# Second half of the tokens in a hybrid attention layer: four column pairs of the input projection in seven block products, the other twelve columns cut into pieces of three matmuls

## The chip, the cores and the metric

The kernel runs on one core of one Trainium2 chip. The metric is the device time of one execution in microseconds (us). Before the change it is 2535.86 us, the median of three runs (2535.32 to 2537.22). One further execution was recorded by the hardware profiler; it took 2533.9 us, of which the recorded span of the program is 2532.2 us.

The engines are named as the profile names them: PE is TensorE (matmuls), PEld its weight loads, DVE is VectorE, ACT is ScalarE, POOL is GpSimd, SP is SyncE, which here only issues DMAs.

## What is computed

One layer of a streaming encoder over 2048 tokens of width 1024, in float32. The parts that matter here:

```python
u = rms_norm(h, g_mix_pre)                      # 2048 x 1024
z = u @ w_in                                    # 1024 x 2816: 22 column blocks of 128
qa, ka, va, qh, fh, ih, gh = split(z, IN_SPLITS)
ya = swa_with_sinks(qa, ka, va, sinks)          # sliding window of 128, 8 heads of 64, sink logits
yh = hgrn2(qh, fh, ih, gh, lb, onorm)           # gated recurrence, 4 heads of 128, chunks of 64
y  = concatenate([ya, yh]) @ w_out
h  = h + rms_norm(y, g_mix_post)
# cross-attention into 256 memory tokens, then a SwiGLU FFN of width 2816, each with its norms
```

In the attention of each head, the softmax runs over the window's scores and one further logit, the sink.

## The kernel before

Every large product is split in three: each float32 operand is the sum of a rounded high part and a low part, and a product is high x high, high x low and low x high. So a block of 128 columns, 1024 deep, for 512 tokens, is 8 x 3 = 24 matmuls of 128x512.

**Stage 1** (`in_first`, lines 471 to 628) normalises the input and projects the first 1024 tokens. Two columns of `w_in` (a pair, from the table `ORDER`) form a 2x2 block problem with the two halves of the depth and the two halves of the tokens. The method `seven` (line 1202) does it in seven products of 12 matmuls instead of eight. It needs seven combinations of the token operand, called T and numbered 1 to 7 (8 where the product is a plain one), each stored as high and low parts in SBUF, and seven combinations of the weights, called S, which `streamed` (line 1132) makes for each pair. The seven T stand in seven slots: four in the pool `big`, three in the pool `t2`. `phases` (line 1286) is the loop over pairs: for each product (a step) it records the matmuls, the results' epilogue, the next S and, where a new set of T is due, half a T at a time. `split2` (line 1027) makes a high part on ACT or POOL and the low part on DVE (line 1038).

After the eleven pairs, stage 1 loads the second 1024 tokens' `u`, splits it into four tiles `u1` (no combinations), and projects one pair, columns 4 and 5 (the keys and values of the attention), plainly, in 96 matmuls.

**The mixing stage** follows. It runs three things side by side: the sliding-window attention `swa` for 16 blocks of 128 tokens, n = 0 to 15; the recurrence `hgrn` for the first 8 blocks; and `in_proj` (line 737), which projects the remaining 20 columns for the second half of the tokens, one column of 48 matmuls after another (`in_cols`, tiles `psg`, `whi`, `wlo`). `swa_front(n)` (line 816) loads queries (`qs`), keys (`kk`) and values (`vr`), makes four banks of scores, and the softmax; `swa_back(n)` (line 882) transposes the probabilities (tile `S` by `ident`), splits them (`pth`, `ptl`) and multiplies by the values. `hgrn_front` writes `atz`, `kt`, `vt`; the tile `W` is the recurrence's state. The back of n-1 is recorded after the front of n. The order of instructions on each engine is set when the program is built, by a list scheduler that knows priorities (the order of recording) and its own estimate of durations; on the chip each engine takes its queue strictly in that order. Columns of `in_proj` are recorded one per block, so the scheduler drops their matmuls wherever it sees PE free.

`kk` has two buffers: the keys of n+1 can be loaded while the scores of n still read theirs. The loads are issued by SP in the order of its queue.

The sink enters the softmax as follows: the row's minimum of the negated scores and the negated sink is taken on DVE (line 864), the exponentials and their sum on ACT (line 868); the sink's own exponential takes one POOL addition (line 871), one ACT exponential (line 872) and another POOL addition (line 874) before DVE takes the reciprocal (line 876).

**The later stages**: the fold of the cross-attention's weights, which runs beside the second half of `hgrn`, then the output projection, cross-attention and FFN, all as `phases` of seven products.

## Time and profile before

| what | value |
|---|---|
| median of three runs | 2535.86 us |
| the profiled execution | 2533.9 us |
| its span | 2532.2 us |
| PE busy | 2493.8 us, 98% of the span, 11942 matmuls |
| DVE busy | 1749.1 us, 69% |
| ACT busy | 1240.7 us, 49% |
| POOL busy | 365.4 us, 14% |
| stage 1 ends, first `psg` matmul of the mixing stage | 269.0 us |
| first score matmul of the mixing stage | 282.1 us |
| last `psg` matmul | 633.0 us |

The span is the time from the first to the last instruction of the program; the execution's own time is 1.7 us longer. A matmul's record overlaps with the next one's, because matmuls are pipelined, so "busy" does not say that PE runs at its peak; the number of matmuls in a window divided by its length says that better. The PE clock that the chip granted is in a column of its own, 1.00 for full speed.

### The profile page before, as it was taken

The page shows a single profiled execution, that of the slowest core. Times are in us where ns is not written, and L with a number is a line of the kernel's source. Part 1 is how long each engine was busy: PE and PEld are TensorE (multiplying, and loading weights), DVE is VectorE, ACT ScalarE, POOL GpSimd, SP SyncE. Part 2 cuts the span into 40 slices and gives each one's busy share as a digit, 9 for nine tenths or more (in the row PEclk, how much of TensorE's full clock was granted, in tenths as well). Part 3 has the DMA queues.
Part 4 walks back from the last instruction along what each step waited for, and adds up shares of the span by engine and source line. Part 5 has one row for each costly group of instructions (what it writes and reads, how often), then busy time and mean ns, then how long its engine had stood idle before and what let it go on. Part 6 is the DMA issues. An engine that isn't in the chain of part 4 may idle for free.

```text
span 2532.2 us, 33939 instructions
## 1 busy us (share of the span) xinstructions
PE 2493.8 (98%) x11942; PEld 2084.7 (82%) x11942; DVE 1749.1 (69%) x2787; ACT 1240.7 (49%) x2582; POOL 365.4 (14%) x540
## 2 busy tenths in 40 slices
PE   9999999999999999999999999999999999999998
PEld 8778888888987788878878888888888888888886
DVE  8896477865556989988866655576566557574766
ACT  5463356654565576566753333353333335443543
POOL 4241244321400111112200000000000000000122
PEclk9999999999999999999999999999999999999999
DMA  7544877785887996858944322254354334565777
GB/s 221 158 158 164 239 198 178 223 270 135 278 298 266 302 335 194 255 175 255 339 164 169 136 76 93 78 196 154 129 208 167 117 127 156 177 184 110 231 169 156
DMA packets 313403, 483.56 MB, mean 191 GB/s; under 512 B 21904, under 2 KB 198032, under 8 KB 313232
## 3 DMA queue, kind: packets, MB, share of 16 engines
q1 hardware_dynamic: 304880, 455.17, 54.1%
q0 software_dynamic: 8352, 26.22, 6.1%
q8 instruction: 94, 1.54, 0.2%
q14 instruction: 77, 0.63, 0.1%
HBM read 305.15 MB, written 176.16 MB: 190 GB/s over the span
## 4 chain that ended last, share of the span: by engine, by line
PE 83%; DVE 5%; DMA 5%; issue 2%; ACT 2%; POOL 1%; SPq 1%; DVEq 0%; POOLq 0%; ACTq 0%
PE psm L1200 22%; PE psm L1198 22%; PE psm L1199 22%; PE psg L158 2%; PE psg L156 2%; PE psg L157 2%; DVE S L1038 1%; DMA y_d<-ys 1%; DVE T L1038 1%; DMA raw<-in_wo_x_dram 1%; DVE sum L1173 0%; DMA pair<-in_x_dram 0%; DMA out_s<-u 0%; SPq L75 0%; ACT junk L1569 0%
## 5 line engine op out<-in xcount | busy, mean ns | idle before, releaser
L1198 PE MATMUL psm<-T,S 128*128 128x512 f32 x2680 | 1034.4, 391 | 12.6 <-ACT part L1213 8.4
L1199 PE MATMUL psm<-T,S 128*128 128x512 f32 x2680 | 1042.6, 390 | 1.2 <-DVE T L1038 1.1
L1200 PE MATMUL psm<-T,S 128*128 128x512 f32 x2680 | 1030.0, 390 | 5.0 <-DVE S L1038 5.0
L1198 PEld LDWEIGHTS psm<-T,S 128*128 128x128 f32 x2680 | 503.1, 188 | 124.8 <-ACT part L1213 13.0
L1200 PEld LDWEIGHTS psm<-T,S 128*128 128x128 f32 x2680 | 503.4, 188 | 112.4 <-DVE S L1038 8.4
L1199 PEld LDWEIGHTS psm<-T,S 128*128 128x128 f32 x2680 | 503.5, 188 | 106.7 <-DVE T L1038 3.0
L1035 ACT ACTIVATE S<-sum 128x512 fp32r<-128x512 f32 (+1 forms) x370 | 224.1, 619 | 374.8 <-PE psm L1200 270.4
L1038 DVE TENSOR_TENSOR S<-sraw,S 128x512 fp32r<-128x512 f32 (+1 forms) x315 | 212.0, 679 | 236.9 <-ACT S L1035 233.7
L1213 ACT ACTIVATE part<-psm 128x512 f32<-128x512 f32 x285 | 168.6, 596 | 253.1 <-PE psm L1200 237.8
L1038 DVE TENSOR_TENSOR S<-sum,S 128x512 fp32r<-128x512 f32 (+1 forms) x388 | 258.0, 673 | 43.9 <-ACT S L1035 40.0
L1035 ACT ACTIVATE S<-sraw 128x512 fp32r<-128x512 f32 (+1 forms) x300 | 184.5, 618 | 110.7 <-PE psm L1200 108.7
L1602 POOL DMA_DIRECT2D y_d<-row x16 | 14.0, 872 | 1077.3 <-DVE row L1784 1015.3
L1038 DVE TENSOR_TENSOR T<-row,T 128x1024 fp32r<-128x1024 f32 (+1 forms) x112 | 130.8, 1183 | 28.3 <-ACT T L1035 26.4
L156 PE MATMUL psg<-u,whi 128*128 128x512 f32 x320 | 127.6, 399 | 0.7 <-DVE z L770 0.5
L157 PE MATMUL psg<-u,whi 128*128 128x512 f32 x320 | 127.3, 398 | 0.0
L158 PE MATMUL psg<-u,wlo 128*128 128x512 f32 x320 | 126.7, 397 | 0.0
L1569 ACT ACTIVATE junk<-row 128x512 f32<-128x512 f32 x160 | 99.6, 624 | 46.3 <-DVE row L1591 19.9
L1035 ACT ACTIVATE T<-row 128x1024 fp32r<-128x1024 f32 (+1 forms) x112 | 113.4, 1031 | 10.6 <-DMA row<-d_s 5.3
L1735 DVE TENSOR_TENSOR row<-psm,part 128x512 f32<-128x512 f32 x66 | 44.0, 687 | 71.3 <-PE psm L1200 71.3
L1038 DVE TENSOR_TENSOR wlo<-raw,whi 128x1024 fp32r<-128x1024 f32 x52 | 65.4, 1258 | 36.0 <-ACT whi L1035 30.9
L1784 DVE TENSOR_TENSOR row<-psm,part 128x512 f32<-128x512 f32 x72 | 49.1, 687 | 49.3 <-PE psm L1200 49.2
L1744 DVE TENSOR_TENSOR part<-psm,part 128x512 f32<-128x512 f32 x66 | 43.7, 687 | 52.2 <-PE psm L1200 52.2
(355 smaller groups left out, 3476.2 us busy)
## 6 DMA issues: line engine op xcount, KB each, us to landing
sraw<-in_w_gate_dram SPq DMA_DIRECT2D x44, 512.0 KB, 3.8
sraw<-in_w_up_dram SPq DMA_DIRECT2D x44, 512.0 KB, 3.6
hid_d<-row SPq DMA_DIRECT2D x44, 512.0 KB, 2.6
sraw<-hid_d SPq DMA_DIRECT2D x32, 512.0 KB, 4.6
sraw<-in_w_in_dram SPq DMA_DIRECT2D x48, 256.0 KB, 3.9
raw<-in_w_in_dram SPq DMA_DIRECT2D x20, 512.0 KB, 6.3
row<-in_w_down_dram SPq DMA_DIRECT2D x20, 512.0 KB, 7.3
row<-d_s SPq DMA_DIRECT2D x20, 512.0 KB, 8.4
```

Source lines behind the costliest of these rows:

```text
L156: nc.tensor.matmul(ps, ah, bh, start=(i == 0), stop=False)
L157: nc.tensor.matmul(ps, ah, bl, start=False, stop=False)
L158: nc.tensor.matmul(ps, al, bh, start=False, stop=(i == n - 1))
L1035: self.nc.scalar.activation(hi, raw, AF.Copy)
L1038: self.nc.vector.tensor_tensor(lo, raw, f32(hi), ALU.subtract)
L1198: nc.tensor.matmul(ps, s[:, 0, k, :], t[:, 0, k, :], start=st, stop=False, **kw)
L1199: nc.tensor.matmul(ps, s[:, 0, k, :], t[:, 1, k, :], start=False, stop=False, **kw)
L1200: nc.tensor.matmul(ps, s[:, 1, k, :], t[:, 0, k, :], start=False, stop=sp, **kw)
L1213: nc.scalar.activation(t, ps, AF.Copy)
L1569: self.nc.scalar.activation(junk, a, AF.Square, scale=float(D) ** -0.5, accum_out=to)
L1735: nc.vector.tensor_tensor(d, a, c, ALU.add)
L1784: nc.vector.tensor_tensor(d, a, b, ALU.add)
```

## The change

Nothing of what the layer computes is changed. Five things are:

1. In stage 1 the second half of the tokens becomes a second job of `phases` with the first five pairs of `ORDER` (`MORE = 5`): columns (4,5), (0,1), (2,3) and (10,6) in seven products each, (11,7) in eight. For that the T of the second half are made: the generator `sums` loads the four blocks of `u` and makes three of the combinations in place on DVE, `operand` hands them to `split2` and makes the last. Each new T takes the slot of the first job's T of the same number. Blocks (0,1) and (1,1) are loaded a second time.
2. `in_proj` keeps twelve columns (12, 8, 13, 9, 14 to 21). It yields after each three matmuls (one step of depth: high x high, high x low, low x high); a method `fill(n)` records n such pieces, each bound to issue after the PE instruction recorded last. 32 pieces run before the mixing stage's first block; then 1 to 2 pieces stand behind each of the four score groups and 2 behind the transposes of each head group. A column's weights are loaded one column ahead.
3. The softmax: the masked scores go to four fixed tiles `scores`, with the negated sink in an extra last column, so the exponential and its sum on ACT include the sink; the POOL additions and the extra exponential are gone.
4. Buffers: `kk` has one buffer instead of two, `qs` three instead of four, `ys` is named with two.
5. The accumulating DMA of the attention's output (POOL queue) is issued one block later.

The core of the diff, with whole hunks left out:

```diff
-                cols = self.in_proj(1, u)
-                next(cols)
-                for _ in range(NPB + 1):
+                cols = self.cols = self.in_proj(1, u)
+                for _ in range(32):
+                    next(cols)
+                self.fills = (1, 1, 1, 1, 2, 2)
+                for i in range(NPB + 1):
                     next(swa)
                     next(hgrn)
-                    next(cols)
+                self.fills = (1, 2, 2, 1, 2, 2)
...
+        more = [("p" if i == self.MORE - 1 else "s",) + self.in_block(*p, 1, (), [], (), False, None)
+                for i, p in enumerate(self.ORDER[:self.MORE])]
...
+        def sums():
+            for k, at in ((7, (1, 1)), (5, (0, 1)), (1, (0, 0)), (2, (1, 0))):
+                second[k] = fetched(*at)
+                yield
+            for d, a, b, op in ((7, 7, 5, ALU.subtract), (5, 5, 1, ALU.subtract), (6, 1, 7, ALU.add)):
...
+                for k in (0, 2):
+                    kk = slice(k, k + 2)
+                    nc.vector.tensor_tensor(second[d][:, kk], second[a][:, kk], second[b][:, kk], op)
+                    yield
+        def operand(i, j, a, n):
+            key = i if j is None else {v: k for k, v in self.BLOCK.items()}[i, j]
+            if key in (3, 8) and not a:
+                second[key] = fetched(i, j)
+            if key == 4:
+                return second[2][:, a:a + n], second[6][:, a:a + n]
+            return second[key][:, a:a + n]
...
-        phases = self.phases([(lambda i, j, a, n: raw[i, j][:, a:a + n, :], 4, blocks, None, {})], T)
+        phases = self.phases([(lambda i, j, a, n: raw[i, j][:, a:a + n, :], 4, blocks, None, {len(blocks) - 2: [sums]}),
+                              (operand, 4, more, True, {})], T)
...
-        for s in range(2):
-            u.append([])
-            for q in range(2):
-                t = self.big.tile([P, 2, 4, 512], F32R, tag="big", name=f"u1_{q}{s}")
...
-                self.mm3(ps, [((S[i + k // 4 * 2][:, 0, k % 4, :], S[i + k // 4 * 2][:, 1, k % 4, :]), u[s][k])
-                              for k in range(KT)])
+        T = {k[1]: t for k, t in T.items() if type(k) is tuple and k[0]}
+        return [[(T[p][:, 0, k, :], T[p][:, 1, k, :]) for p in ps for k in range(4)] for ps in ((1, 2), (8, 3))]
...
+    def fill(self, n):
+        for _ in range(n):
+            with self.queued(self.traced(mybir.EngineType.PE)):
+                next(self.cols, None)
...
-                self.mm3(ps, [((w[i][0][:, k, :], w[i][1][:, k, :]), u[s][k]) for k in range(KT)])
+            for k, (bh, bl) in enumerate(u[s]):
+                ah, al = w[0][:, k, :], w[1][:, k, :]
+                nc.tensor.matmul(ps, ah, bh, start=(k == 0), stop=False)
+                nc.tensor.matmul(ps, ah, bl, start=False, stop=False)
+                nc.tensor.matmul(ps, al, bh, start=False, stop=(k == KT - 1))
+                if k < KT - 1:
+                    yield
...
-            q = ph.tile([P, 4, P], F32R, tag="qs", name=f"qs{n}_{g}", bufs=4)
+            q = ph.tile([P, 4, P], F32R, tag="qs", name=f"qs{n}_{g}", bufs=3)
...
-        kk = ph.tile([P, 2, 2, M], F32R, tag="kk", name=f"kk{n}", bufs=2)
+        kk = ph.tile([P, 2, 2, M], F32R, tag="kk", name=f"kk{n}", bufs=1)
...
+                self.fill(self.fills[2 * g + i2])
...
-            se = self.small("w_se", 4)
-            nc.gpsimd.tensor_tensor(se, self.sink[:, 4 * g:4 * g + 4], mn, ALU.add)
-            nc.scalar.activation(se, se, AF.Exp)
-            dn = self.small("w_dn", 4)
-            nc.gpsimd.tensor_tensor(dn, den, se, ALU.add)
             rd = self.small("w_rd", 4)
-            nc.vector.reciprocal(rd, dn)
+            nc.vector.reciprocal(rd, den)
...
+            self.fill(self.fills[4 + g])
...
+                if first and queue[0][0]:
+                    free = next(s for s in slots if s[2] == where[queue[0][1]])
```

How the change moves instructions is shown at two places. The first is DVE's queue at the end of stage 1, where the T of the second half come in. The first row, `pair<-psm,part` of line 694, is the epilogue of product 3 of the first job's last pair, the same work in both kernels (line 685 in the changed one). Before, this is what stands behind it (the `u` row is two halves of a tile):

```order
L694 TENSOR_TENSOR pair_2169<-psm_2118,part_2150 128x512
L1038 TENSOR_TENSOR u_01_2242<-pair_1948,u_01_2242 128x1024 x2
L1038 TENSOR_TENSOR S_2261<-sraw_2252,S_2261 128x512
L707 SCALAR_TENSOR_TENSOR pair_2169<-th_2171,pair_2169 128x512
L694 TENSOR_TENSOR pair_2169<-psm_2096,part_2131 128x512
```

In the changed kernel the same epilogue row opens a stretch of 26 rows, up to the first half of T_2302, the tile of product 2, the sixth of the seven. Its end reads:

```order
L1038 TENSOR_TENSOR T_2222<-pair_2223,T_2222 128x1024
L1038 TENSOR_TENSOR S_2384<-sraw_2104,S_2384 128x512
L1178 TENSOR_TENSOR sum_2474<-sraw_2275,sum_2451 128x512
L1038 TENSOR_TENSOR T_2222<-pair_2223,T_2222 128x1024
L1038 TENSOR_TENSOR S_2366<-sraw_2104,S_2366 128x512
L1038 TENSOR_TENSOR T_2271<-pair_1972,T_2271 128x1024
L1038 TENSOR_TENSOR T_2302<-pair_2037,T_2302 128x1024
```

On PE, that tile is asked for by the 57th matmul counted from the second job's first (twelve of these still belong to the first job's last product), ahead of the last ones of product 3 (T_2222):

```order
L1205 MATMUL psm_2303<-T_2222,S_2320 128x512
L1203 MATMUL psm_2303<-T_2222,S_2320 128x512
L1203 MATMUL psm_2278<-T_2271,S_2343 128x512
L1203 MATMUL psm_2390<-T_2302,S_2366 128x512
L1204 MATMUL psm_2303<-T_2222,S_2320 128x512
```

So nine halves of T stand in this stretch of DVE's queue, where before it held halves of `u` tiles, and on PE single products now ask for them in turn.

The second place is SP's queue in the mixing stage, at the loads for one block of attention (`kk` is loaded in two halves of 64 partitions, `qs_0` and `qs_1` are the queries of the two head groups; the brackets name what a row waits for, PE or an earlier transfer). Before, at n = 3, the query load waits for PE, the key load for no engine:

```order
L75 DMA raw_3922<-in_w_in_dram 128x1024 [waits DMAHW0_49,DVE_49]
L75 DMA qs_1_3170<-zq_d 64x4x128 [waits DMAHW1_49,PE_49]
L75 DMA qs_1_3170<-zq_d 64x4x128 [waits DMAHW2_49]
L75 DMA kk_3173<-zk_d 64x4x256 [waits DMAHW3_49]
L75 DMA kk_3173<-zk_d 64x4x256 [waits DMAHW4_49]
L75 DMA qq_3339<-z_d 128x4x128 [waits DMAHW5_49,PE_49]
```

In the changed kernel, at n = 10, the key load itself waits for PE, that is for the last score matmul of n = 9, which reads the only `kk` buffer:

```order
L75 DMA sg_5066<-z_d 128x4x128 [waits DMAHW4_49,DMAHW1_49]
L75 DMA qs_1_5272<-zq_d 64x4x128 [waits DMAHW5_49,PE_49]
L75 DMA qs_1_5272<-zq_d 64x4x128 [waits DMAHW6_49]
L75 DMA kk_5275<-zk_d 64x4x256 [waits DMAHW7_49,PE_49]
L75 DMA kk_5275<-zk_d 64x4x256 [waits DMAHW0_49]
L75 DMA qs_0_5437<-zq_d 64x4x128
L78 DMA y_d<-sg_5066 128x512 [waits DMAHW2_49,DVE_49]
```

PE's queue behind those scores holds what is left of block n = 9 before the first score of the next block. The end of that stretch, for n = 10 to n = 11 (`pth`, `ptl` by `vst` are the value products, `vr` the transposed values):

```order
L899 MATMUL psh_5395<-pth_00_5376,vst_4915 128x512
L899 MATMUL psh_5426<-pth_10_5406,vst_4915 128x512
L900 MATMUL psh_5395<-ptl_00_5377,vst_4915 128x512
L899 MATMUL psh_5395<-pth_01_5385,vst_5121 128x512
L840 MATMUL pss_5448<-ident,vr_5446 128x128
L900 MATMUL psh_5395<-ptl_01_5386,vst_5121 128x512
L859 MATMUL pst_5456<-kk_5443,qs_0_5437 128x256
```

Between the last score of one block and the first of the next there are now, on PE, only the pieces and the back of the block before; a load that starts at the one has to land before the other.

More of the change, by code (lines that the diff above doesn't have):

```diff
@@ L250, in prologue @@
                             next(phases)
-                next(cols)
+                for _ in range(8):
+                    next(cols, None)
                 next(fold)
@@ L662, in stream, with out @@
         def stream(kind):
-            for _ in range(3):
-                next(iter(get), None)
             return self.streamed(load, 4, kind)
-        def out(i, j, a, b):
+        def out(i, j, a, o):
             c0 = (ca, cb)[i] * P
@@ L737, in in_proj @@
     def in_proj(self, b, u):
-        order = [c for p in self.ORDER for c in p]
+        order = [c for p in self.ORDER for c in p][2 * self.MORE:]
         e1 = None
-        for c in order[2:]:
-            e1 = self.in_cols(b, u, [c], e1)
+        w = self.wcols(self.I["w_in"], order[0] * P)
+        for c, d in zip(order, order[1:] + [None]):
+            cur = self.in_cols(b, u, c, e1, w)
+            next(cur)
             yield
-    def in_cols(self, b, u, cols, e1):
+            if d is not None:
+                w = self.wcols(self.I["w_in"], d * P)
+            e1 = yield from cur
@@ L1302, in phases @@
         held = 7 if first else -1
-        slots = [("A", -2, i) for i in range(4)] + [("B", held if i == 2 else -1, i) for i in range(3)]
-        T, keep = {}, [{} for _ in jobs]
+        slots = [("A", -2, i) for i in range(4)] + [("B", held if i == 6 else -1, i) for i in range(4, 7)]
+        T, keep, where = {}, [{} for _ in jobs], {}
         current, left = [None], {}
@@ L1346, in half @@
                 n, p, _ = k = queue.pop(0)
+                where[p] = free[2]
                 slots.remove(free)
```

165 lines of the change are left out of this document (72 added, 93 removed).

## The prediction

> **What bounds the kernel now.** I read the page first, for the busy shares and the chain that ended last.
>
> ```profile
> span 2532.2 us, 33939 instructions
> PE 2493.8 (98%) x11942; PEld 2084.7 (82%) x11942; DVE 1749.1 (69%) x2787; ACT 1240.7 (49%) x2582; POOL 365.4 (14%) x540
> PE 83%; DVE 5%; DMA 5%; issue 2%; ACT 2%; POOL 1%; SPq 1%; DVEq 0%; POOLq 0%; ACTq 0%
> ```
>
> PE is the bound: 83% of the chain is PE. So a matmul that is left out is worth its pitch, the time from one start to the next, as long as nothing else comes to end last. I then cut the span into windows, for that pitch and for the stages that the change touches (columns: window, its length, then busy time and instruction count of each engine, granted PE clock, share of the DMA engines, GB/s).
>
> ```profile
> core 0: us, PE busy (x) PEld busy (x) DVE busy (x) ACT busy (x) POOL busy (x), PEclk, DMA share, GB/s
> 1300.00:1650.00 350.00, 350.00 (x1546) 289.92 (x1545) 201.46 (x304) 125.03 (x221) 0.00 (x0) 1.00 0.32 112
> 110.00:115.00 5.00, 1.98 (x7) 1.64 (x8) 5.00 (x7) 3.94 (x6) 0.86 (x3) 0.94 0.43 105
> 115.00:120.00 5.00, 5.00 (x18) 3.97 (x17) 3.03 (x5) 1.12 (x2) 1.12 (x2) 0.72 0.27 80
> 224.20:269.00 44.80, 44.24 (x195) 36.32 (x194) 26.75 (x37) 17.30 (x25) 8.53 (x11) 1.00 0.50 164
> 269.00:300.00 31.00, 30.53 (x168) 26.24 (x167) 12.39 (x45) 10.52 (x40) 8.26 (x14) 1.00 0.97 259
> 300.00:460.00 160.00, 159.81 (x948) 139.95 (x947) 109.91 (x281) 96.00 (x290) 63.17 (x99) 1.00 0.68 184
> 460.00:540.00 80.00, 79.81 (x433) 67.87 (x432) 66.18 (x166) 43.83 (x128) 23.34 (x38) 1.00 0.91 283
> 540.00:597.00 57.00, 56.51 (x302) 47.79 (x301) 37.93 (x113) 33.67 (x101) 12.26 (x27) 1.00 0.60 163
> ```
>
> In an undisturbed stretch of the later stages 1546 matmuls of 128x512 take 350 us: **0.226 us each**. From 224 to 269, the end of stage 1, 195 stand in 44.8 us, 0.230 each, so PE loses little there. In the mixing stage, 269 to 597, PE shows idle time of 0.47 + 0.19 + 0.19 + 0.49 = 1.3 us in all. There is next to nothing to win from waits in the places that the change rebuilds; what it can win is matmuls. Last, who made PE wait, from 90 to 270 and from 270 to 610 (us in total, times, the longest):
>
> ```profile
> PE psm L1198 <- ACT part L1213: 6.5, 5, 3.1
> ...
> PE psh L903 <- DVE ptl L898: 0.7, 2, 0.5
> PE psh L859 <- ACT ys L904: 0.5, 1, 0.5
> PE pst L859 <- DMA kk<-zk_d: 0.5, 1, 0.5
> ```
>
> **The change part by part.** *Matmuls.* Four pairs go from eight products to seven, 12 matmuls each: 4 x 12 = 48 fewer of 128x512, and the built order of PE agrees (9736 against 9784, all other shapes alike). 48 x 0.226 = **-10.9 us**. Moving 384 column matmuls from the mixing stage into stage 1 is by itself worth nothing.
>
> *T of the second half.* DVE makes the seven low parts and the differences while the first job's last pair runs. I add up its queue from the epilogue of product 3 to the first half of the tile of product 2, the 26 rows named above: nine halves of T (128x1024) and 17 rows of 128x512.
>
> ```profile
> start us, us, engine line op out<-in xcount [idle before <-releaser]
> 224.38 1.29 DVE L694 TENSOR_TENSOR pair<-psm,part 128x512 f32<-128x512 f32 x2 [1.75 <-PE psm L1200]
> 229.19 2.35 DVE L1038 TENSOR_TENSOR u<-pair,u 128x1024 fp32r<-128x1024 f32 x2
> 240.44 0.68 DVE L694 TENSOR_TENSOR pair<-psm,part 128x512 f32<-128x512 f32 x1
> ...
> 244.54 0.39 PE L156 MATMUL psm<-u,S 128*128 128x512 f32 x1
> ```
>
> Two rows of 512 take 1.29 us with 0.69 for the last, so 0.60 from start to start; two of 1024 take 2.35, so 1.18. The stretch is 9 x 1.18 + 17 x 0.60 = 20.8 us. It cannot begin before 240.4, since its first row waits for PE in both kernels, so the tile is there at 261.2. The second job's first matmul stands where the first plain one stands now, at 244.54; the tile is asked for 56 matmuls later, at 244.54 + 56 x 0.226 = 257.2. **+4.0 us.** After that DVE has slack again, since PE's next new tile is asked for 47 matmuls (10.6 us) on and DVE's rows up to it are ten. The lower end is 0, if DVE finds rows ready in another rhythm than I assume; the upper end is 8, if it stands idle once more for as long as ACT's high parts (2.0 us for two halves) hold it twice.
>
> *One more pair of forget gate and query in seven products*, (10,6). The five waits for ACT's copies fall into stage 1; without the longest they are (6.5 - 3.1) / 4 = 0.85 us. **+0.9 us**, between 0 and 3.1 + 1.2 (below).
>
> *Start of the mixing stage.* The loads of the attention wait on SP until stage 1's pools are free. Now 48 matmuls (10.9 us) cover that; then 96 will (21.7), while the last pair's decay chain (ACT, DVE and POOL) comes ahead of it. I cost it at 0; if the cover is short, by as much as DVE's stretch above is short of its own, it costs up to 4.
>
> *The mixing stage's density.* It becomes 384 x 0.226 = 87 us shorter, 328 to 241. DVE worked 12.4 + 109.9 + 66.2 + 37.9 = 226.4 us there, so it would fit even if none of its work left. The DMA engines were busy for 0.97 x 31 + 0.68 x 160 + 0.91 x 80 + 0.60 x 57 = 246 us, and moved some 69 MB; eight columns' weights and results (16 transfers of 0.5 MB) leave, 12%, so 216 of 241. That fits, at 90%; I cost it at 0 and keep the other end as a rival. The POOL additions that leave the softmax were waited for by DVE, not by PE; nothing for them.
>
> *One key buffer.* This is the added wait. The keys of block n+1 are requested when the last score of n is done, in two halves on SP, and behind them in SP's queue stand queries, results and weights.
>
> ```profile
> L75 SPq DMA_DIRECT2D kk<-zk_d x32: 573/614/1507, 276.9 to 553.3; - x32
> ...
> DMA to landing us min/median/max: 3.8/6.4/7.7
> ...
> 341.81 0.60 PE L994 MATMUL psh<-ident,on 128*128 128x128 f32 x4
> 342.25 0.39 PE L976 MATMUL psh<-vt,atz 128*128 128x128 f32 x2
> ```
>
> The second half is issued 0.6 us after the first and lands 6.4 us later (median of 32; 3.8 to 7.7): 7.0 us (4.4 to 8.3). What PE has to do meanwhile I count from its new order, a filler or value matmul at 0.227, four transposes at 0.44 (341.81 to 342.25), a pair of recurrence matmuls at 0.22. From block 0 to 1: 3 fillers, 8 pairs of `atz` and state, 4 pairs for `W`, 2 wide pairs: 0.7 + 1.8 + 0.9 + 0.5 = about 4.0 us. From 1 to 2: 12 fillers, 20 transposes, 4 value products and the rest, 6.4 us. From 10 to 11 and three more like it: 15 fillers, 16 transposes, 5 value products, 3.4 + 1.8 + 1.1 + 0.1 = 6.4 us. At the other handovers it is 8.5 us or more. So at the median (7.0 - 4.0) + 5 x (7.0 - 6.4) = **+6.0 us**; at the quickest landing 0.4; at the slowest 4.3 + 5 x 1.9 = 13.8. I take the median, because the DMA engines stay about as busy as when it was measured. The Trainium skill, "DMA: Bandwidth & Descriptors", section "Anatomy of one DMA", fits one transfer as 2.0 us plus bytes / 436 GB/s, which as an estimate is 2.6 us for 256 KB. By that rule the landing would be hidden at every handover, and the sum would be 6 us lower; the trace disagrees for these scattered loads, with 3.8 us at the least.
>
> *Sum:* -10.9 + 4.0 + 0.9 + 6.0 = 0.0 us against the profiled execution's 2533.9 us. The median of the runs stands 2.0 above it; I put the same difference on the median: **2536 us**.
>
> **The rivals.**
>
> *The covers hold, and most of the 48 matmuls show.* The same key loads by window, from 269 to 300, 300 to 460, 460 to 540 and 540 to 597:
>
> ```profile
> DMA to landing us min/median/max: 4.2/4.8/7.2
> ...
> DMA to landing us min/median/max: 4.5/6.7/7.7
> ...
> DMA to landing us min/median/max: 4.6/6.6/7.2
> ...
> DMA to landing us min/median/max: 3.8/6.1/7.3
> ```
>
> For it: PE waited 1.3 us in the whole mixing stage, and the keys of the first blocks landed in 4.8 us at a share of 0.97, so the handover with the thinnest cover may be the one with the quickest load. Against it: behind 300 the median is 6.1 to 6.7, whatever the share. With the quickest landing the time is 2535.9 - 10.9 + 4.0 + 0.9 + 0.4 = **2530 us**; with DVE's stretch hidden too, 2526.
>
> *The single key buffer decides, and it gets slower.* Place: the first score of each block, lines 859 and 860, waiting for `kk`. Price as above with a landing L: L + 0.6 - 4.0 once and L + 0.6 - 6.4 five times. With the other terms at -6.0 it turns the sum positive from L = 6.4 on, and past 0.2% (5.1 us, about what a measurement of this kernel can tell from no change) from L = 7.25 on. At 7.7: -6.0 + 13.8 = +7.8, **2544 us**. For it: landings of 7.2 to 7.7 stand in each of the windows, and the share rises to 0.90. It has an aggravation: behind the one wait of 3.1 us the granted clock was 0.72 (18 matmuls in 5 us instead of 22, 0.9 to 1.2 us lost). The Trainium skill, "TensorE: Matmul & The Clock Gate", section "HAM oscillation", says that an idle PE of more than about 3.4 us halves the clock until it is busy again; by that rule, which the window at 115 supports at 3.1 us, the first handover would cost a microsecond more.
>
> *DMA-bound in the middle.* From 460 to 540 the DMA engines worked 73 of 80 us, with the weights for the output projection's sums. There four blocks become 19 us shorter while a tenth of the transfers goes: 66 us of transfers in 61 of PE. If the queues can't spread that, +5, **2541 us**.
>
> *The change does not do what it says* is excluded for the matmuls by the built order; only their time can differ.
>
> **How the numbers follow.** No measurable change, 2531 to 2541: 0.37. Faster, by the first rival: 0.33. Slower, by the second or third: 0.30. The ends of the unknown costs give -10.9 + 0 + 0 + 0.4 = -10.5 and -10.9 + 4.0 + 2.0 + 13.8 + 1.2 = +10.1, so **2526 to 2547** with a little for their coming together; some 0.15 to 0.2 lies outside. The likeliest case's own range is 2531 to 2541.
>
> **What would show it.** Right: stage 1 ends some 80 us later than now (4 x 84 matmuls, and 5 us); a wait of PE on DVE's T of about 4 us before that; waits of lines 859 and 860 for `kk<-zk_d`, the longest at the second block; `se` and `dn` gone from POOL. Wrong: no wait for `kk`, or PE waiting in the mixing stage for `pth`, `ptl` or S on ACT and DVE instead, which would mean that latency between engines, and not the key buffer, replaces the fillers that left; or a start of the mixing stage that waits for the loads.

## The result and the profile after

The changed kernel takes 2558.4 us (median; 2552.95 to 2560.96) against 2536.54 us before in the same session: 1.0085 of it, 95% interval 1.0072 to 1.0098. It is slower by some 22 us. The profiled execution took 2560.96 us, the longest of the four; that of before, at 2533.9 us, was shorter than the runs of its median, so the two traces differ by 5 us more than the medians do.

The lines of the page of after that answer to those shown of before (span, busy time of the engines, the chain that ended last):

```profile
span 2559.2 us, 33903 instructions
PE 2496.7 (98%) x11894; PEld 2083.2 (81%) x11894; DVE 1798.0 (70%) x2855; ACT 1260.3 (49%) x2585; POOL 349.5 (14%) x480
PE 77%; DMA 7%; DVE 7%; issue 3%; ACT 3%; POOL 2%; SPq 1%; DVEq 0%; POOLq 0%; ACTq 0%
```

PE is still "98% busy", with 48 matmuls fewer, so the page's first line hides what happened. The chain shows it: PE's share falls from 83% to 77%, and DMA and DVE take the place. The windows show where. First the kernel before, from the first score to the end of the attention, then the same stretch after, and pieces of it (columns as in the prediction):

```profile
280.00:600.00 320.00, 318.65 (x1817) 275.31 (x1815) 228.13 (x603) 185.83 (x561) 104.04 (x172) 1.00 0.74 208
```

```profile
core 0: us, PE busy (x) PEld busy (x) DVE busy (x) ACT busy (x) POOL busy (x), PEclk, DMA share, GB/s
348.00:372.00 24.00, 24.00 (x112) 20.12 (x110) 15.45 (x23) 11.57 (x17) 14.76 (x21) 1.00 0.58 178
368.00:620.00 252.00, 226.55 (x1329) 194.67 (x1328) 187.87 (x533) 147.94 (x464) 66.48 (x83) 0.96 0.81 218
...
380.00:400.00 20.00, 15.79 (x89) 13.77 (x88) 11.54 (x41) 9.12 (x37) 4.68 (x6) 0.83 0.76 172
440.00:460.00 20.00, 16.16 (x91) 13.80 (x89) 18.16 (x42) 9.99 (x35) 7.77 (x8) 0.84 1.02 294
540.00:560.00 20.00, 20.00 (x113) 17.01 (x111) 12.45 (x44) 12.11 (x42) 1.05 (x1) 1.00 0.60 173
```

Before, PE stood idle for 1.35 of 320 us. After, it stands idle for 25.45 of 252 us, and the mean clock of the stretch is 0.96. No other engine is full over the stretch: DVE goes from 71% to 75%, the DMA engines from 0.74 to 0.81. For a while the DMA engines are (1.02 from 440 to 460), but that was so before as well (1.03 from 500 to 540), and there PE lost only 0.2 us. The start of the mixing stage (348 to 372) has no idle time. PE's waits from 340 to 640, the nine largest of sixteen (us in all, times, the longest):

```profile
PE pss L900 <- DVE ptl L894: 3.3, 2, 1.7
PE psh L962 <- DVE sg L992: 3.0, 1, 3.0
PE pst L859 <- issue: 2.8, 1, 2.8
PE psh L859 <- ACT ys L901: 2.4, 1, 2.4
PE psh L900 <- DVE ptl L894: 2.3, 2, 1.7
PE psh L946 <- POOL k L943: 2.2, 1, 2.2
PE pst L859 <- DMA kk<-zk_d: 1.8, 1, 1.8
PE psh L935 <- DVE W L964: 1.4, 1, 1.4
PE psh L973 <- ACT vt L953: 1.0, 1, 1.0
```

These are waits on three engines and on DMAs, 25.1 us with the seven that are not shown, and no line holds a sixth of it. By what ended them, DVE has 11.5 us, ACT 5.8, POOL 3.2 and the keys 4.6 (counting the 2.8 of "issue", explained below). That is the reading: not one thing is late, everything is, a little, one after the other.

For the comparison of runs I add up one quantity from each trace: the time from each matmul's start to the next one's, less the undisturbed pitch of its width (0.2268 us for 512 elements, 0.1195 for 256, 0.1625 for 192, 0.109 for 128), from 2 us before the first score to 30 us after the last. It holds waits and slow clock together, and is called **lost time** below. It is 6.7 us before and 42.9 us after (29.2 of it in steps that are over 0.35 us too long). Outside the mixing stage PE's loss hardly changed: ahead of it 17.3 before and 20.5 after, behind it 27.4 and 25.6. So -10.9 (48 matmuls) + 36.2 + 3.2 - 1.8 = +26.7, and the two spans differ by 27.0. By block: before, blocks 3 to 7 took 22 us each and held 55 to 57 matmuls of 128x512; after, blocks 2 to 8 took 17.3 to 23.9 us and held 31 to 33, with 15 to 17 us of work for PE.

### The profile page after: what moved, and what is told of

It is laid out like the page before. It is cut to its first block, busy times and chain, and to the rows that moved or that the text cites. A ratio compares the mean times of both kernels' runs of the same rounds, so it can differ in the third digit from the quotient of the medians.

```text
span 2559.2 us, 33903 instructions
## 1 busy us (share of the span) xinstructions
PE 2496.7 (98%) x11894; PEld 2083.2 (81%) x11894; DVE 1798.0 (70%) x2855; ACT 1260.3 (49%) x2585; POOL 349.5 (14%) x480
## 4 chain that ended last, share of the span: by engine, by line
PE 77%; DMA 7%; DVE 7%; issue 3%; ACT 3%; POOL 2%; SPq 1%; DVEq 0%; POOLq 0%; ACTq 0%
PE psm L1203 22%; PE psm L1205 22%; PE psm L1204 22%; DVE T L1038 1%; DVE S L1038 1%; PE psg L759 1%; PE psg L758 1%; PE psg L757 1%; DMA kk<-zk_d 1%; DMA raw<-in_wo_x_dram 1%; DMA u<-in_w_out_dram 1%; POOL pair L693 1%; SPq L75 1%; DMA y_d<-sg 1%; DMA sg<-z_d 1%
## 5 line engine op out<-in xcount | busy, mean ns | idle before, releaser
L1203 PE MATMUL psm<-T,S 128*128 128x512 f32 x2824 | 1090.0, 391 | 15.7 <-ACT part L1218 10.0
L1204 PE MATMUL psm<-T,S 128*128 128x512 f32 x2824 | 1099.0, 390 | 1.5 <-DVE T L1038 1.4
L1205 PE MATMUL psm<-T,S 128*128 128x512 f32 x2824 | 1085.7, 390 | 3.8 <-DVE S L1038 3.8
L1203 PEld LDWEIGHTS psm<-T,S 128*128 128x128 f32 x2824 | 530.6, 188 | 134.7 <-ACT part L1218 15.0
L1205 PEld LDWEIGHTS psm<-T,S 128*128 128x128 f32 x2824 | 530.7, 188 | 117.2 <-DVE S L1038 6.9
L1204 PEld LDWEIGHTS psm<-T,S 128*128 128x128 f32 x2824 | 530.8, 188 | 112.6 <-DVE T L1038 3.8
L1038 DVE TENSOR_TENSOR S<-sraw,S 128x512 fp32r<-128x512 f32 (+1 forms) x327 | 220.9, 682 | 237.5 <-ACT S L1035 234.4
L1218 ACT ACTIVATE part<-psm 128x512 f32<-128x512 f32 x297 | 175.9, 597 | 266.2 <-PE psm L1205 250.3
L1038 DVE TENSOR_TENSOR S<-sum,S 128x512 fp32r<-128x512 f32 (+1 forms) x404 | 269.5, 676 | 44.6 <-ACT S L1035 40.8
L1580 ACT ACTIVATE junk<-row 128x512 f32<-128x512 f32 x160 | 99.6, 624 | 46.8 <-DVE row L1602 20.7
L1038 DVE TENSOR_TENSOR wlo<-raw,whi 128x1024 fp32r<-128x1024 f32 x44 | 55.5, 1262 | 41.9 <-ACT whi L1035 36.3
L1178 DVE TENSOR_TENSOR sum<-sraw,sraw 128x512 f32<-128x512 f32 (+1 forms) x101 | 70.3, 696 | 16.1 <-DMA sraw<-in_w_in_dram 12.4
L757 PE MATMUL psg<-T,whi 128*128 128x512 f32 x192 | 79.9, 416 | 1.0 <-POOL whi L1037 1.0
L759 PE MATMUL psg<-T,wlo 128*128 128x512 f32 x192 | 76.9, 400 | 0.0
```

Of the source, the lines that this page charges most:

```text
L757: nc.tensor.matmul(ps, ah, bh, start=(k == 0), stop=False)
L759: nc.tensor.matmul(ps, al, bh, start=False, stop=(k == KT - 1))
L1038: self.nc.vector.tensor_tensor(lo, raw, f32(hi), ALU.subtract)
L1178: nc.vector.tensor_tensor(t, a, b, op)
L1203: nc.tensor.matmul(ps, s[:, 0, k, :], t[:, 0, k, :], start=st, stop=False, **kw)
L1204: nc.tensor.matmul(ps, s[:, 0, k, :], t[:, 1, k, :], start=False, stop=False, **kw)
```

## The experiments

Every run is compared with the kernel before on the same chip; the interval of each ratio is 0.0010 to 0.0019 to either side, some 2.5 to 5 us. The theories: **missing work** (PE has too little else to do while other engines finish a step), **places** (the pieces are bound to fixed places, where PE's waits are not), **buffers** (one key buffer), **softmax** (its new form).

### One part undone at a time

Pieces free, first:

```diff
         for _ in range(n):
-            with self.queued(self.traced(mybir.EngineType.PE)):
-                next(self.cols, None)
+            next(self.cols, None)
```

> The pieces are no longer bound to issue behind the PE instruction recorded last; the scheduler places them. If the pinned places cause the 41 us that PE loses in the mixing stage: most of the loss goes, 2530 to 2540 us. If there is too little other work left in each block (24 to 30 matmuls of 128x512 beside 47 to 57 before), or if the softmax or the buffers cause it: 2555 to 2562 us, the waits stay where they are.

2568.75 us, 1.0121 of before (1.0106 to 1.0136): slower still, and outside both forecasts. Freed, the scheduler took 36 to 82 matmuls of 128x512 into each of the blocks 0 to 8, which lost little, and blocks 10 to 14 were left with 7 to 9 and lost 4 to 7 us each. Waits appear where the matmuls are gone.

The softmax of before, then with the key and query buffers of before as well (the two buffer lines are in the second run alone):

```diff
...
+            se = self.small("w_se", 4)
+            nc.gpsimd.tensor_tensor(se, self.sink[:, 4 * g:4 * g + 4], mn, ALU.add)
+            nc.scalar.activation(se, se, AF.Exp)
+            dn = self.small("w_dn", 4)
+            nc.gpsimd.tensor_tensor(dn, den, se, ALU.add)
             rd = self.small("w_rd", 4)
-            nc.vector.reciprocal(rd, den)
+            nc.vector.reciprocal(rd, dn)
...
-            q = ph.tile([P, 4, P], F32R, tag="qs", name=f"qs{n}_{g}", bufs=3)
+            q = ph.tile([P, 4, P], F32R, tag="qs", name=f"qs{n}_{g}", bufs=4)
...
-        kk = ph.tile([P, 2, 2, M], F32R, tag="kk", name=f"kk{n}", bufs=1)
+        kk = ph.tile([P, 2, 2, M], F32R, tag="kk", name=f"kk{n}", bufs=2)
```

> The softmax as before the change (two POOL additions and an exponential more per head group, scores in place), all else as changed. If the rewritten softmax costs time: at least 8 us under the changed kernel, 2550 or less. If too little work, pinned places or buffers cause the loss: 2556 to 2564, since the longer sink chain only adds latency.

2556.63 us, 1.0076 (1.0061 to 1.0091), 18.1 us over before where the changed kernel has 21.9: no difference that the intervals can tell.

> As the run with the old softmax, and two key buffers and four query buffers as before the change (the room comes from the four score tiles that are gone). If the single key buffer is the main cause, as the prediction has it: 15 us or more under the run with the old softmax alone, 2545 or less. If it only costs the two waits named for keys and queries (3.0 + 2.0 us and the slow clock behind them): 4 to 9 us under it. If too little work decides: under 5 us, since other engines are late next.

2555.03 us, 1.0069 (1.0054 to 1.0084), only 1.6 us under the run with one key buffer. No wait on keys is left, and this stands in its place (PE's waits from 360 to 640):

```profile
PE pst L887 <- DVE w_mn L858: 10.0, 5, 3.9
PE pss L887 <- DVE w_mn L858: 2.3, 3, 1.7
```

The transposes of a block now wait for DVE's scores. Why DVE was late at 420 is in DVE's and POOL's timelines (start, duration, instruction, idle time before it and what ended it):

```profile
416.38 0.44 DVE L934 COPY_PREDICATED atz<-cmask,psh 128x256 f32<-128x256 int32 x1
420.16 0.18 DVE L870 RECIPROCAL w_rd<-w_dn 128x4 f32<-128x4 f32 x1 [3.33 <-POOL w_dn L868]
```

```profile
417.74 1.06 POOL L902 DMA_DIRECT2D y_d<-ys  x1 [3.50 <-DMA y_d<-ys]
418.48 0.97 POOL L941 TENSOR_TENSOR k<-k,G 128x256 f32<-128x256 f32 x1
419.06 0.55 POOL L865 TENSOR_TENSOR w_se<-sink,w_mn 128x4 f32<-128x4 f32 x1
```

POOL issues the accumulating output DMA only when the first half of that output has landed, and the sink's addition stands behind it in POOL's queue. Then ACT, POOL and DVE follow in turn, and DVE's next scores stand behind the reciprocal. In the changed kernel this way does not exist, since the sink is a column of the scores; its place is taken by other waits. Both forms of the softmax lose about the same.

Two key buffers in the changed kernel:

```diff
-        kk = ph.tile([P, 2, 2, M], F32R, tag="kk", name=f"kk{n}", bufs=1)
+        kk = ph.tile([P, 2, 2, M], F32R, tag="kk", name=f"kk{n}", bufs=2)
...
-        ys = ph.tile([P, 2, 512], F32, tag="ys", name=f"ys{n}", bufs=2)
+        ys = ph.tile([P, 2, 512], F32, tag="ys", name=f"ys{n}", bufs=1)
...
+            if low is not None:
+                low()
+                low = None
             yield
-        low()
```

(`low` issues the accumulating output DMA.)

> The changed kernel with two key buffers; the room comes from ys (one buffer, as before the change), and so the accumulating output DMA stands where it stood before. If the key buffer is only the wait that happens to be last and too little work per block decides: no wait on keys, other waits take their place, 2550 to 2558 us. If the key buffer decides: 2545 or less.

2573.56 us, 1.0150 (1.0134 to 1.0167), 15 us slower than the changed kernel, and outside both forecasts. The waits on keys are gone, but `ys` with one buffer waits for its output DMA, and ACT's copy into it for that (PE's waits from 360 to 650, the two largest):

```profile
PE psh L859 <- ACT ys L901: 6.6, 3, 4.3
PE pst L859 <- DVE w_mn L865: 3.5, 1, 3.5
```

Less work for DVE:

```diff
-            rd = self.small("w_rd", 4)
-            nc.vector.reciprocal(rd, den)
-            for i in range(4):
-                a = S[2 * g + i // 2][:, i % 2, o:M]
-                nc.vector.tensor_scalar_mul(a, a, rd[:, i:i + 1])
```

> The changed kernel without the reciprocal and the multiplication of the exponentials by it (the attention is left unnormalised, which changes the result): 8 rows of 0.4 us fewer on DVE per block, and a shorter way from the scores to the transposes. If DVE's queue is the main thing that PE waits for: the loss of the mixing stage falls by half or more, 2530 to 2542 us. If keys, ACT and POOL take over: 2548 to 2558.

2557.65 us, 1.0083 (1.0067 to 1.0100): DVE is busy for 1757.3 us in place of 1798.0, 2.5 us less per block, and nothing is gained. Lost time is 40.7 us; PE waits for `kk`, `ys`, `pth`, `ptl` and `sg` instead.

### The buffers and the softmax at the old density

```diff
-        kk = ph.tile([P, 2, 2, M], F32R, tag="kk", name=f"kk{n}", bufs=2)
+        kk = ph.tile([P, 2, 2, M], F32R, tag="kk", name=f"kk{n}", bufs=1)
```

(in the kernel before, and `qs` at three)

> The kernel before with one key buffer and three query buffers, nothing else changed. If a single key buffer only costs where little work of PE stands between the last score of a block and the first of the next (before: 47 to 57 matmuls of 128x512 per block): within 4 us of the kernel before, waits on keys under 3 us in all. If the single buffer costs by itself: 8 us or more over the kernel before.

2541.95 us, 1.0019 (1.0010 to 1.0029): 5.3 us over before, between the two forecasts. The largest wait, 3.5 us, is for queries, not keys.

> As the run with one key buffer in the kernel before, and the new softmax with its four score tiles as well. If too little work per block is the cause of the loss: as that run, within 3 us, the softmax and the buffers together cost under 5 us at the old density. If the new softmax costs by itself: 5 us or more over that run.

2540.74 us, 1.0017 (1.0008 to 1.0027): 4.1 us. The new softmax costs nothing that the intervals can tell; it pays for its four tiles with the buffers, and these cost 4 to 5 us. Neither explains 22, let alone 33 (22 and the 10.9 us of matmuls that were saved).

### More columns in the mixing stage

```diff
-                self.fills = (1, 1, 1, 1, 2, 2)
+                self.fills = (2, 2, 2, 2, 2, 2)
...
-                self.fills = (1, 2, 2, 1, 2, 2)
+                self.fills = (2, 3, 3, 2, 2, 2)
...
-    MORE = 5
+    MORE = 3
```

> Only three pairs of the second half in stage 1 (two in seven products, one in eight), sixteen columns left, 12 pieces per block in the first half of the mixing stage and 13 in the second, pinned as in the change; 24 matmuls more than the changed kernel (5.4 us). If too little work per block decides: PE's loss in the mixing stage falls from 41 us to 12 or less, 2530 to 2538 us. If the pinned places decide whatever the density: the loss stays over 30, 2553 to 2565. If the single key buffer decides: the waits on keys go as the cover grows, other waits stay, about 2555.

2556.17 us, 1.0071 (1.0054 to 1.0088): not the recovery that missing work alone forecast, but inside what the pinned places forecast. Lost time fell from 42.9 to 32.3 us with 40 to 51 matmuls per block from block 1 on, and 12.4 us of the waits were for keys.

The same with the two key buffers of above:

> Three pairs in stage 1, 12 to 13 pieces per block, and two key buffers with ys at one. The run with three pairs had 12.4 us of waits on keys among 22.9 us of waits. If work per block and key buffer act together: the waits on keys go and little comes in their place, 2538 to 2546 us. If other waits take their place at this density as well: 2550 or more.

2552.19 us, 1.0064 (1.0047 to 1.0081); the waits on keys went, 7.7 us for `ys` came. Lost time 26.8.

Three pairs with the free pieces of above, first with the buffers and softmax of the change, then with those of before:

> Three pairs in stage 1, sixteen columns left, the pieces no longer bound to a place, buffers and softmax as changed. The free pieces ran out early with twelve columns (blocks 0 to 8 held 36 to 82 matmuls of 128x512 and lost little, blocks 10 to 14 held 7 to 9 and lost 4 to 7 us each); with sixteen they should last. If work that can be put where PE would wait is what counts: 2538 to 2545 us, and the loss in the mixing stage 10 to 16 us, most of it keys. If the place does not matter: 2553 to 2558, as the pinned one with three pairs.

2559.26 us, 1.0094 (1.0077 to 1.0111). A miss, with a lost time of 36.4 us: the free pieces ran out early again, blocks 12 to 15 held 7 to 9 matmuls and lost 4.5 to 7.3 us each.

> Three pairs in stage 1 and free pieces, with the softmax, the key, query and output buffers and the output DMA of before. If free pieces and a second key buffer remove the loss at this density: 24 matmuls fewer than before (5.4 us) less 3 us for the waits in stage 1, 2532 to 2540 us. If the mixing stage cannot do with 64 pieces fewer in any arrangement: 2545 or more.

2553.85 us, 1.0068 (1.0052 to 1.0085). With the softmax, the buffers and the output DMA of before and the pieces free, 5.4 us of matmuls are saved, and still the run is 18 us over; lost time is 29.4 us. Here too the last two blocks had 8 and 9 matmuls. None of these versions comes near the kernel before.

### Matmuls taken away, and given back

The kernel before with matmuls taken out, and nothing else touched:

```diff
-                self.mm3(ps, [((w[i][0][:, k, :], w[i][1][:, k, :]), u[s][k]) for k in range(KT)])
+                self.mm3(ps, [((w[i][0][:, k, :], w[i][1][:, k, :]), u[s][k]) for k in range(KT - 3)])
```

> The kernel before, with only five of eight steps of depth in each of the twenty columns of the mixing stage (which changes the result): 360 matmuls fewer, 81.5 us at 0.2265, about 38 of 128x512 per block in place of 56; softmax, buffers, order and free placing stay as before. If missing matmuls alone make PE wait: 20 to 37 us of it come back as waits, 2475 to 2492 us. If another part of the change is the cause: nearly all of it shows, 2455 to 2463.

2499.23 us, 0.9850 (0.9833 to 0.9866). 81.5 us of matmuls went, 37.5 us of time: **44 us came back**, more than either forecast. Lost time is 55.8 us in place of 6.7. The windows of this run show it in one column (PE busy):

```profile
350.00:420.00 70.00, 68.79 (x407) 59.88 (x406) 60.54 (x139) 48.41 (x129) 35.24 (x50) 1.00 0.80 225
505.00:550.00 45.00, 31.75 (x145) 25.07 (x144) 31.09 (x109) 27.52 (x89) 6.30 (x17) 0.76 0.66 162
```

Where the scheduler had matmuls (46 to 59 of 128x512 per block), PE is busy for 98% of the window. Where they had run out (7 or 8 per block), PE is busy for 71% at a clock of 0.76, with DVE at 69% and the DMA engines at 0.66. Blocks 11 to 13 held 5.5 us of work for PE and took 12.8 to 13.4 us; block 14, with as much, took 9.1, and the last blocks of the runs with free pieces took 9.9 to 13.8. That is what a late block costs when PE has next to nothing to put beside it. Of the 55.8 us, 36 lie in blocks 10 to 15. So the run shows what blocks cost that have run out of matmuls; blocks thinned evenly to the 31 to 33 of the changed kernel it does not show.

The changed kernel with more matmuls in each piece, one more (the line written twice) and two more (the diff):

```diff
-                nc.tensor.matmul(ps, ah, bl, start=False, stop=False)
+                for _ in range(3):
+                    nc.tensor.matmul(ps, ah, bl, start=False, stop=False)
```

> The changed kernel with a fourth matmul in each piece (the product high by low is added twice in the twelve columns, which changes the result): 192 matmuls more, 43.5 us at 0.2265. If the waits of PE come from too little work between the steps of other engines: a good part of the new matmuls falls into the waits, 2572 to 2588 us. If the waits are a fixed toll of each block: 2598 to 2603.

2589.95 us, 1.0208 (1.0191 to 1.0225), a little above the forecast of missing work. Of 43.5 us, 11 to 12 fell into waits: lost time 30.1.

> The changed kernel with five matmuls in each piece in place of three (high by low added three times, which changes the result): 384 matmuls more, 87.0 us at 0.2265, as many as the kernel before has in the mixing stage. One extra matmul per piece cost 31.6 of 43.5 us. If missing matmuls make PE wait: the loss goes on falling, from 42 to 20 us or less, 2613 to 2625 us. If a toll of the blocks is left that matmuls do not fill: the second one costs its full 43.5, 2632 to 2637.

2633.51 us, 1.0381 (1.0365 to 1.0397). The second extra matmul cost its full 43.5 us; lost time stays at 30.1. So missing work alone is not all of it.

Nor is what is left a toll of each block. By block it is 9.7 us in block 3, 5.1 in block 0 and 4.4 in block 5, while seven of the sixteen blocks lose 0.3 us or less. Block 3, on DVE and then on PE:

```profile
447.82 0.09 DVE L866 DVE_READ_ACCUMULATOR2_ANT w_mn<- 128x1 f32 x1
451.32 1.23 DVE L1088 TENSOR_TENSOR u<-u,x 128x1024 f32<-128x1024 f32 x1 [3.42 <-DMA u<-in_w_out_dram]
...
455.50 0.68 DVE L895 TENSOR_TENSOR ptl<-pss,pth 128x512 fp32r<-128x512 f32 x1
```

```profile
456.23 0.79 PE L901 MATMUL pss<-ptl,vst 128*128 128x512 f32 x1 [3.72 <-DVE ptl L895]
```

DVE stands 3.42 us for a load of the output projection's weights, whose sums it makes beside the attention; the block's reciprocal and its low parts stand behind that in its queue, and PE waits for them. The run with two key buffers below loses 9.1 us in the same block, behind a wait of 3.09 us for the same load. In the kernel before, DVE waits for such a load too (3.0 us), and there PE had matmuls to do.

The same with free pieces, and the same with two key buffers:

> Five matmuls per piece (high by low added three times, which changes the result) and pieces that are not bound to a place; all else as changed. If the fixed places are the rest of the cause: the loss in the mixing stage falls from 30 to 15 us or less, 2612 to 2621 us. If they are not: 2628 to 2637, as the pinned one with five matmuls (2633.5).

2619.93 us, 1.0324 (1.0307 to 1.0341). Lost time 15.7 us, about that of the kernel before with one key buffer, three query buffers and the new softmax (15.0). PE's waits from 380 to 700, pinned and then free:

```profile
PE pst L860 <- DMA kk<-zk_d: 3.8, 1, 3.8
PE pss L901 <- DVE ptl L895: 3.7, 1, 3.7
PE psh L947 <- POOL k L944: 2.0, 2, 1.4
```

```profile
PE pss L900 <- DVE ptl L894: 1.6, 1, 1.6
PE pst L900 <- DVE ptl L894: 1.3, 1, 1.3
PE psh L900 <- DVE ptl L894: 1.1, 3, 0.6
...
PE pst L859 <- DMA kk<-zk_d: 0.4, 1, 0.4
```

> Five matmuls per piece (high by low added three times, which changes the result), fixed places, two key buffers and one output buffer as in the earlier run. If the single key buffer is the rest of the cause: 10 us or more under the pinned one with five matmuls, 2623 or less. If other waits take its place: 2626 to 2640.

2626.35 us, 1.0346 (1.0327 to 1.0364), 8 us less over its kernel before than the pinned run with one key buffer, the intervals just apart; its runs spread from 2619.3 to 2628.9, and it lies at the edge of the forecast of other waits. Lost time 19.0.

### Side by side

"Over" is the difference to the kernel before in the same session; "without matmuls" has the matmuls taken off that the run has more or less than before, at 0.2265 us each. Lost time is that of the profiled execution, which lies up to 5 us from the median.

| run | matmuls of 128x512 | over, us | without matmuls, us | lost time in mixing, us |
|---|---|---|---|---|
| the change: 3 per piece, pinned | -48 | 21.9 | 32.8 | 42.9 |
| 3 per piece, free | -48 | 30.2 | 41.1 | 50.8 |
| 4 per piece, pinned | +144 | 54.1 | 21.5 | 30.1 |
| 5 per piece, pinned | +336 | 96.8 | 20.7 | 30.1 |
| 5 per piece, free | +336 | 82.4 | 6.3 | 15.7 |
| 5 per piece, pinned, two key buffers | +336 | 88.8 | 12.7 | 19.0 |
| before, thinned | -360 | -37.5 | 44.0 | 55.8 |
| before, one key buffer, three query buffers | 0 | 5.3 | 5.3 | 13.6 |

The cause is shown from both ends. Taking matmuls out of the kernel before makes a loss without any other edit. Giving them back to the changed kernel and letting the scheduler place them removes 26.5 of its 32.8 us. Each of the two alone removes 12 us (more matmuls) or makes it 8 us worse (free places): free places help only while there is something to place, and more matmuls help only where PE waits. The remaining 6 us is about what the buffers cost at the old density (4 to 5 us); no run with five matmuls, free pieces and two key buffers was made, so that this is the rest is not shown.

## Why the prediction was wrong, point by point

**The step that failed is the density of the mixing stage, costed at 0.** It added up DVE's 226.4 us and the DMA engines' 216 us and found that both fit into 241 us. They do, and the stage was still not so short: a block is a chain (scores on PE, minimum on DVE, exponentials on ACT, transposes on PE, split on ACT and DVE, values on PE, copy on ACT), beside it the recurrence has one of its own, and each engine takes its queue in order. Late blocks left with some 5.5 us of work for PE, and without the recurrence, still took 9 to 14 us, and a sum of busy times does not contain that. The 1.3 us of waits before were read as proof that nothing was to be lost there; they were so few because some 48 matmuls of other work per block, placed freely, covered the handovers. The term measured +36 us with the key buffer's, against 0 + 6.

**48 matmuls, -10.9.** The count is right, and in stage 1 the price as well: stage 1 ends at 348.4, against 269.0 + 336 x 0.2268 = 345.2, and 1.9 of the 3.2 us between them are ACT's copies (below). But moving 384 column matmuls out of the mixing stage was costed as "by itself worth nothing". Moved, they no longer cover anything: a matmul taken from the kernel before returned 37.5 / 81.5 = 0.46 of its pitch.

**T of the second half, +4.0: none.** DVE's timeline and PE's at the tile of product 2:

```profile
260.89 2.35 DVE L1038 TENSOR_TENSOR T<-pair,T 128x1024 fp32r<-128x1024 f32 x2
```

```profile
259.88 0.94 PE L1203 MATMUL psm<-T,S 128*128 128x512 f32 x3
260.66 0.40 PE L1204 MATMUL psm<-T,S 128*128 128x512 f32 x1
```

The stretch of DVE's queue took 21.4 us (241.9 to 263.2), as reckoned (20.8). PE came to the tile 3.1 us later than reckoned (260.3 for 257.2, the third matmul in the row of L1203), which would still have left a wait of some 3 us. But that matmul is a product of two high parts, and ACT makes those. The product with T's low part (L1204 on that tile) stands 21 matmuls later, at 265.2, when DVE had been done for 2 us. The step read the first use of a tile as the first use of both its parts.

**One more pair with ACT's copies, +0.9.** ACT's copies cost 8.4 us in six waits after, 6.5 in five before: +1.9. Right in kind. **Start of the mixing stage, 0.** Right: no idle time from 348 to 372.

**One key buffer, +6.0.** As a wait it was sized well: at the second block 2.85 us (3.0 forecast; the profile puts it down to "issue", and the keys, whose second half was issued at 379.69 and landed at 387.55, are what comes last before the score at 387.64) and once more 1.8 us, 4.6 in all. As a price it was wrong, since at this density its removal gave 1.6 us with the old softmax (within the intervals) and with the new one, `ys` back at one buffer, cost 15: another wait stood behind it. The prediction holds a rule of the Trainium skill, "DMA: Bandwidth & Descriptors", section "Anatomy of one DMA", against this term; that fit is given there for DMAs that GpSimd issues, and the keys are issued by SP.

**The rivals.** The slower rival had the sign; its mechanism, a landing of 7.7 us at every handover, was not it (the median landing was 5.0 us after, 9.9 at the longest, and keys made PE wait twice). The third, full DMA engines in the middle, was tested by no run; it may have a part in the block-3 loss above, behind a load that DVE waits for at a DMA share of 1.1. The sentence on what would be wrong named the true case: PE waiting for `pth`, `ptl` and S on ACT and DVE, latency in place of the fillers that left. It had been given no price and no chance. The row for it was at hand, the number of matmuls per block that hid the handovers.

**The range.** It is narrower than its terms. Beside the key buffer its upper end adds 4.0, 2.0 and 1.2, where the text gives upper ends of 8 for T, 4.3 for the pair and 4 for the start. With these it would reach 2555, still short of the 2558.4 measured, since the density stands in it at 0.

What stays open: whether twelve columns, placed where PE waits and spread so that they last to the end, would do better; with twelve or sixteen columns freed pieces ran out each time, and a mixture of free and bound ones was not tried. How long the chain of one of the blocks 1 to 8 is by itself, with the recurrence beside it, no run shows.

## What to carry to other kernels

Work that is moved off a stage takes its cover with it. Ahead of such a move, ask how long a block would take if the bound engine had nothing else to do (here 9 to 14 us for a late block, with 5.5 us of PE's own work), not only whether each engine's busy time fits. The cheapest test is to thin the filler in the old kernel: it shows in one run what the freed time is worth. And when many waits on several engines are each small, undoing one part gains next to nothing; change the cover instead, its amount and its places together.

## What was not expected of the hardware

The granted clock fell after waits shorter than the 3.1 us of the prediction's row. PE after the wait of 3.01 us at 454, one 128x512 matmul after another:

```profile
457.82 0.78 PE L757 MATMUL psg<-T,whi 128*128 128x512 f32 x1
458.39 0.63 PE L758 MATMUL psg<-T,whi 128*128 128x512 f32 x1
458.82 0.63 PE L759 MATMUL psg<-T,wlo 128*128 128x512 f32 x1
...
460.52 0.40 PE L900 MATMUL pss<-ptl,vst 128*128 128x512 f32 x1
460.76 0.40 PE L899 MATMUL pst<-pth,vst 128*128 128x512 f32 x1
```

They stand 0.43 us apart until 460.5 and 0.24 after. Four such stretches of 3 to 7 us, behind waits of 2.85, 2.2, 3.0 and 1.8 us, cost some 8 us in all; waits of 1.6 to 2.4 us at 434, 475, 577 and 595 were followed by none. The Trainium skill, "TensorE: Matmul & The Clock Gate", section "HAM oscillation", has PE gaps of more than about 3.4 us as what slows the clock; in this mixing stage none was as long.

The granted clock of the traces shows what went ahead of the drops instead. It changes only on a grid of 3.41 us: here it is 0.50 from 385.42 to 392.25, 419.55 to 422.97, 453.69 to 460.51 and 535.61 to 539.02. The step ahead of each drop, the first drop itself, and a step behind which the clock stayed (the wait at 595):

```profile
382.01:385.42 3.41, 1.41 (x9) 0.93 (x7) 2.85 (x6) 0.89 (x8) 2.99 (x4) 1.00 1.06 266
385.42:392.25 6.83, 4.61 (x15) 4.06 (x16) 1.80 (x8) 1.98 (x8) 0.00 (x0) 0.50 0.61 100
416.14:419.55 3.41, 1.20 (x9) 1.04 (x9) 3.41 (x7) 0.43 (x1) 0.89 (x2) 1.00 1.01 392
450.27:453.69 3.42, 1.07 (x7) 0.57 (x5) 2.47 (x3) 3.05 (x14) 2.59 (x4) 1.00 1.02 379
532.19:535.61 3.42, 1.58 (x14) 1.42 (x13) 3.42 (x8) 1.14 (x8) 2.71 (x4) 1.00 1.07 303
593.64:597.05 3.41, 1.59 (x9) 1.42 (x10) 1.45 (x2) 3.26 (x9) 0.75 (x2) 1.00 0.17 43
```

PE was busy for 0.41, 0.35, 0.31 and 0.46 of the four steps ahead of the drops, and for 0.47 of the last one. Over the 18 traces of this case, 20 us at each end left out, each of the 61 full-clock steps in which PE was busy for less than 0.45 was followed by one at 0.50, and none in which it was busy for more than 0.59; between the two both occur. So gaps within one step add up (the longest single one ahead of a drop was as short as 0.8 us), and a wait counts for less when the border of two steps cuts it, as it does the wait of 2.36 us that ended at 595.46 (0.54 us of it lie ahead of 593.64).
